# Sums of weights for a seven-product MLP: from VectorE to accumulating DMAs on GpSimd's queue

## The chip, the cores and the metric

The kernel runs on one core of one Trainium2 chip. The metric is the device time of one execution in microseconds (us). Time before: 1537.05 us, the median of three runs (1533.11 to 1542.72).

## The reference, cut to what matters

The whole program is one inference step of a two-layer decoder trunk: a layer with an mLSTM/GLA mixer, a layer with a Mamba-2 mixer, and after each mixer an MLP. 512 prompt tokens and 32 sample tokens (8 sequences of 4) are computed together as 544 columns. The change lies in the MLP, which runs twice:

```python
D_MODEL = 1024; D_FF = 4 * D_MODEL
def _mlp(x, w1, w2):
    return jnp.square(jax.nn.relu(x @ w1)) @ w2
x = _layernorm(DN_ALPHA * x + _mlp(x, P['mlp_w1'][l], P['mlp_w2'][l]), ...)
```

All numbers are float32.

## The kernel before, in words

Activations lie transposed, features on the 128 partitions and tokens along the free axis, in two halves of 272 tokens (TH). A float32 product is made from three float32r products: every operand is split into a high part (a cast to float32r, on ScalarE) and a low part (the rest, a subtraction on VectorE), and TensorE adds high*high, high*low and low*high. For weights the high part is `whi` and the low part `wlo`; a wlo instruction is called lo below.

The 32 blocks of w1 (128 hidden rows each) are done in two ways. Blocks 0 to 5 are done one by one (`dense`, L350). Blocks 6 to 31 are done in 13 **pairs** (m, m+1) by a seven-product scheme (Strassen and Winograd): a pair of weight blocks is a 2x2 matrix a11, a12 (from block m, its two halves over the 1024 features) and a21, a22 (from block m+1), the activations are a 2x2 matrix b11, b21, b12, b22 (feature halves by token halves), and seven products of the size 128 x 512 x 272 replace eight. `quarter` (L498) makes one product: 12 matmuls of 272 columns. `pair` (L556) makes the seven in the order a11, s2, s3, s1, a22, a12, s4 into four PSUM banks: pa (a11, then a12 added), pb (s2), pc (s3, then a22 added), pe (s1, then s4 added). Between them ScalarE copies pa into z (L564), VectorE adds z and the other banks (L567 to L584: z, c22, c21, c12), and `act` (L548) makes Relu and Square on ScalarE and splits the result into hh and hlo, the input of the second matmul.

s1 to s4 are sums of the four weight quarters, made once for each pair in `_pair` (L180): SP's queue loads both blocks (512 KB each) into two buffers wraw; VectorE makes four sums into `wsum` (L191 to L194, each 128 x 512); then four splits follow (L202 the high part on ScalarE, L203 lo on VectorE): a11|a12, s1|s2, s3|s4, a22. `wsum` has one buffer (bufs=1), so the sums of a pair wait until VectorE has read s3|s4 of the pair before. The sums t1 to t4 of activations are made once for each MLP in `take_sums` (L519).

The list `MLP` (L39) sets the order of the work on TensorE: `out` groups of the second matmul (blocks of w2, `dense`, added to the residual by VectorE at L393 or L395) stand between the pairs. Between pairs 8 and 10 and between 10 and 12 there is a short group of 48 matmuls (about 7 us), between the later ones, from 12 to 28, a group of 96 (12 us), and pair 30 follows pair 28 directly. TensorE's order is written out by hand; on the other engines a scheduler at build time orders the instructions. Weights are asked for ahead by `next` (L211): five buffers of whi and wlo, and one lent, so that a pair is split while the pair before it runs. Every engine executes its own queue in order, so a waiting instruction holds all that stand behind it. GpSimd's queue has no instruction in the MLP stages but the sums for LayerNorm (L402, L404: lns) at their ends.

Of the kernel before, what the change touches and what calls it, by code (L numbers as in the profile page):

```python
# [9 lines left out]
F32 = mybir.dt.float32  # L10
F32R = mybir.dt.float32r
U32 = mybir.dt.uint32
AF = mybir.ActivationFunctionType
ALU = mybir.AluOpType
# [3 lines left out]
P = 128  # L18
D = 1024
KT = 8  # L20
# [95 lines left out]
class WeightStream:  # L116
# [63 lines left out]
    def _pair(self, phase, src1, src2):  # L180


        nc = self.nc
        V = nc.vector
        r = []
        for src in (src1, src2):
            r.append(self.raw.tile([P, KT, P], F32, tag="wraw", name="wraw"))
            nc.sync.dma_start(out=r[-1], in_=src)
        sr = self.pairs.tile([P, 4, 4, P], F32, tag="wsum", name="wsum", bufs=1)
        a11, a12, a21, a22 = r[0][:, :4], r[0][:, 4:], r[1][:, :4], r[1][:, 4:]  # L190
        V.tensor_tensor(sr[:, 0], a21, a22, ALU.add)  # L191
        V.tensor_tensor(sr[:, 1], sr[:, 0], a11, ALU.subtract)
        V.tensor_tensor(sr[:, 2], a11, a21, ALU.subtract)
        V.tensor_tensor(sr[:, 3], a12, sr[:, 1], ALU.subtract)  # L194
        out = []
        for x in (r[0], sr[:, 0:2].rearrange("p s k c -> p (s k) c"), sr[:, 2:4].rearrange("p s k c -> p (s k) c"), a22):
            n = x.shape[1]
            kw = {} if n == KT else dict(bufs=1)
            pool = self._pool(phase) if n == KT else self.pairs
            hi = pool.tile([P, n, P], F32R, tag="whi" if n == KT else "w4h", name="whi", **kw)  # L200
            lo = pool.tile([P, n, P], F32R, tag="wlo" if n == KT else "w4l", name="wlo", **kw)
            self.cut[0] = nc.scalar.copy(hi, x).ins  # L202
            self.cut[1] = nc.vector.tensor_tensor(lo, x, hi.bitcast(F32), ALU.subtract).ins  # L203
            out += [(hi[:, k:k + 4], lo[:, k:k + 4]) for k in range(0, n, 4)]
        return dict(zip(("a11", "a12", "s1", "s2", "s3", "s4", "a22"), out))

# [21 lines left out]
def trunk_kernel(ctx, tc, a, stages=("ab", "mlp0", "ssd", "mlp1")):  # L228
    nc = tc.nc
    V, S, G, TE = nc.vector, nc.scalar, nc.gpsimd, nc.tensor  # L230
    cst = ctx.enter_context(tc.tile_pool(name="cst", bufs=1))
# [16 lines left out]
    for st in stages:  # L248
# [10 lines left out]
        else:  # L259
# [3 lines left out]
            for kind, m, *r in MLP:  # L263
                if kind == "pair":
                    ws.plan(st, "pair", a["mlp_w1"][l, m], a["mlp_w1"][l, m + 1])
                else:
                    k, n = m % 8, r[0]
# [8 lines left out]
    ones = cst.tile([P, P], F32, name="ones")  # L276
    V.memset(ones, 1.0)
    epsc = cst.tile([P, 1], F32, name="epsc")
# [3 lines left out]
    def split(hi, lo, src):  # L282
        i = S.copy(hi, src)  # L283
        V.tensor_tensor(lo, src, hi.bitcast(F32), ALU.subtract)  # L284
        return i.ins
# [36 lines left out]
    def launch(gen, lane="norm"):  # L322
        lanes.setdefault(lane, []).append([next(gen), gen])
# [183 lines left out]
    def mlp(l, phase_, outer, xp, out):  # L507

        own = outer.enter_context(ExitStack())
        pool = outer.enter_context(tc.tile_pool(name=phase_, bufs=1, reuse_waits="tile"))
        tp = own.enter_context(tc.tile_pool(name="t" + phase_, bufs=1, reuse_waits="tile"))
        ws.lend(own.enter_context(tc.tile_pool(name="hlt" + phase_, bufs=HLM, reuse_waits="tile")), phase_, HLM)
        ws.pairs = tp
        bt = {}

        def take_sums():  # L519
            b11, b21, b12, b22 = xf[0][:, :4], xf[0][:, 4:], xf[1][:, :4], xf[1][:, 4:]  # L520
            tr = xp.tile([P, KT, TH], F32, tag="lnq", name="tsum", bufs=1)
            ta, tb = tr[:, :4], tr[:, 4:]
            for n in ("t1", "t2", "t3"):
                bt[n] = [tp.tile([P, 4, TH], F32R, name=n + x, bufs=1) for x in "hl"]
            V.tensor_tensor(ta, b12, b11, ALU.subtract)
            V.tensor_tensor(tb, b22, b12, ALU.subtract)
            split(*bt["t1"], ta)
            split(*bt["t3"], tb)
            V.tensor_tensor(ta, b22, ta, ALU.subtract)
            split(*bt["t2"], ta)  # L530
            V.tensor_tensor(tb, b21, ta, ALU.subtract)

            bt["t4"] = [xh[1][:, :4], xl[1][:, :4]]
            split(*bt["t4"], tb)
            bt["b11"], bt["b21"], bt["b22"] = ([x[h][:, k:k + 4] for x in (xh, xl)] for h, k in ((0, 0), (0, 4), (1, 4)))

        hid = {}

        def place(m):
            if m not in hid:  # L540
                hid[m] = (pool.tile([P, T], F32R, tag="hh", name="hh", bufs=8),
                          pool.tile([P, T], F32R, tag="hlo", name="hlo", bufs=8))
            return hid[m]

        def hr():
            return pool.tile([P, TH], F32, tag="hr", name="hr", bufs=6)

        def act(m, hf, x, r=None):  # L548
            c0, c1 = HALVES[hf]
            h = place(m)  # L550
            r = hr() if r is None else r
            S.activation(r, x, AF.Relu)
            S.activation(r, r, AF.Square)
            split(h[0][:, c0:c1], h[1][:, c0:c1], r)

        def pair(m):  # L556
            w = ws.next()
            pa, pb, pc, pe = (x[:, :TH] for x in (psd.tile([P, 512], F32, tag="d", name="psd"), pm("psd"),
                                                  psd.tile([P, 512], F32, tag="d", name="psd"), pm("psd")))
            hp = tc.high_priority  # L560
            z, c22, c21, c12 = (hr() for _ in range(4))
            quarter(w["a11"], bt["b11"], pa, True)
            with hp():
                S.copy(z, pa)  # L564
            quarter(w["s2"], bt["t2"], pb, True)
            with hp():
                V.tensor_tensor(z, z, pb, ALU.add)  # L567
            quarter(w["s3"], bt["t3"], pc, True)
            with hp():
                V.tensor_tensor(c22, z, pc, ALU.add)  # L570
            quarter(w["s1"], bt["t1"], pe, True)
            with hp():
                V.tensor_tensor(c22, c22, pe, ALU.add)
                act(m + 1, 1, c22, c22)
            quarter(w["a22"], bt["t4"], pc, False)
            with hp():
                V.tensor_tensor(c21, z, pc, ALU.add)
                act(m + 1, 0, c21, c21)
            quarter(w["a12"], bt["b21"], pa, False)
            with hp():  # L580
                act(m, 0, pa)
            quarter(w["s4"], bt["b22"], pe, False)
            with hp():
                V.tensor_tensor(c12, z, pe, ALU.add)  # L584
                act(m, 1, c12, c12)

        def hrhs(m):
            def rhs(k, hf):
                c0, c1 = HALVES[hf]
                return hid[m + k][0][:, c0:c1], hid[m + k][1][:, c0:c1]  # L590
            return rhs

        phase(HEADM, xrhs, KT, act, head=HEADM)
        take_sums()
        for kind, m, *r in MLP:
            if kind == "pair":
                if m == 30:
                    ws.lend(None, None, 0)
                pair(m)
                continue  # L600
            n, blocks = r
            if kind == "last":
                own.close()
                ws.lend(outer.enter_context(tc.tile_pool(name="hlx" + phase_, bufs=HLX, reuse_waits="tile")), phase_, HLX)
                end = None if out is None else lambda: last_layernorm(2 * l + 1, xp, out)
                phase(8, hrhs(m), n, residual(False, xp, end), tail=TAIL,
                      after=lambda hf: launch(layernorm(hf, 2 * l + 1, xp, out)) if end is None or hf == 0 else None)
# [12 lines left out]
            if blocks[-1][-1] == 7:  # L620
                for k in range(m, m + n):
                    del hid[k]
# [1155 lines left out]
    n = 0  # L1778
    spill, ahead = a["xT"], None
    left = ctx.enter_context(ExitStack())  # L1780
    while n < len(stages):
        st = stages[n]
        src = spill
        with ExitStack() as stk:
            if st == "ssd":
# [5 lines left out]
                with tc.tile_pool(name="ssd", bufs=1, reuse_waits="tile") as pool:  # L1791
# [4 lines left out]
                    with tc.manual_schedule(engines={mybir.EngineType.PE}):  # L1796
                        out = ssd(pool, ypool, dram, right, ahead, consts)
# [161 lines left out]
```

## Time and profile before

| | |
|---|---|
| median of three runs | 1537.05 us |
| the profiled execution | 1528.88 us, its span 1527.2 us, granted TensorE clock 0.992 |
| TensorE (PE) busy | 1485.8 us, 97% |
| VectorE (DVE) busy | 1091.9 us, 72% |
| ScalarE (ACT) busy | 794.9 us, 52% |
| GpSimd (POOL) busy | 235.8 us, 15% |
| DMA | 172.10 MB, mean 113 GB/s |
| pairs of the first MLP on TensorE | 369 to 636 us |
| pairs of the second MLP on TensorE | 1196 to 1464 us |

How to read the rows that the prediction shows. A row of the timeline has the start in us, the duration in us, the engine, the line, the operation, out<-in with the shape, and in brackets the idle time of the engine just before it and what ended it. Matmuls are pipelined: each row has 0.29 us, but one starts every 0.125 us, so a quarter of 12 takes 1.5 us and a pair of 84 takes 10.5 us. A row of the waits has the waiting engine and line, what it waited for, us in total, times, and the longest. Busy time does not say what a faster engine is worth; that is read from who waits, in the stage.

### The profile page before, as it was taken

The numbers are of one execution on the slowest core, as the hardware profiler recorded it, in microseconds if no ns is written. First come the engines' busy times: TensorE is split into PE (matmuls) and PEld (weight loads), VectorE is DVE, ScalarE is ACT, GpSimd is POOL, SyncE is SP. The second block draws the span as 40 slices with busy tenths as digits, with TensorE's granted clock in tenths as the row PEclk, the third lists the DMA queues.
The fourth block names the chain that finished last, engine by engine and source line by source line (L and its number), as shares of the span: only waits on it lengthen the run. The fifth ranks groups of instructions, "written<-read, shape, count | busy, mean of one in ns | idle before, by whom it ended". The sixth has DMA issues, their size and how long they took to land.

```text
span 1527.2 us, 29115 instructions
## 1 busy us (share of the span) xinstructions
PE 1485.8 (97%) x11611; PEld 1434.4 (94%) x11611; DVE 1091.9 (72%) x2004; ACT 794.9 (52%) x1727; POOL 235.8 (15%) x298
## 2 busy tenths in 40 slices
PE   8999999999999999999999999999999999999997
PEld 7999999899999999999888788989999999999996
DVE  4974476676776677667899988777678677676656
ACT  5644447374444444536786675554347345345343
POOL 0510322010000000022454444420020000000000
PEclk9999999999999999999999999999999999999998
DMA  6321213403333232425457767364222332333221
GB/s 218 96 69 42 101 46 97 174 23 107 99 99 97 84 97 83 142 76 176 118 132 251 228 188 237 97 195 152 72 73 70 94 90 92 97 91 91 69 84 59
DMA packets 81200, 172.10 MB, mean 113 GB/s; under 512 B 9240, under 2 KB 35736, under 8 KB 80808
## 3 DMA queue, kind: packets, MB, share of 16 engines
q1 hardware_dynamic: 52248, 141.20, 29.7%
q10 hardware_dynamic: 26032, 18.29, 4.5%
q0 software_dynamic: 2784, 10.75, 1.8%
q8 instruction: 91, 1.49, 0.4%
q14 instruction: 45, 0.37, 0.1%
HBM read 153.48 MB, written 16.73 MB: 111 GB/s over the span
## 4 chain that ended last, share of the span: by engine, by line
PE 80%; DVE 10%; ACT 4%; DMA 3%; issue 2%; SPq 0%; POOL 0%; ACTq 0%; DVEq 0%
PE psd L361 53%; PE psd L504 17%; DVE wlo L167 2%; ACT whi L166 1%; PE num L749 1%; DVE acc L1442 1%; DMA h0n<-h0n 1%; PE yp L1548 1%; ACT xf L440 1%; PE gs L979 1%; PE it L1595 1%; DVE h0n L1608 1%; PE sp L1526 1%; DMA wraw<-mlp_w 1%; PE ip L1523 1%
## 5 line engine op out<-in xcount | busy, mean ns | idle before, releaser
L361 PE MATMUL psd<-xh,whi 128*128 128x272 f32 x1504 | 447.9, 298 | 9.7 <-ACT xh L283 5.0
L361 PE MATMUL psd<-xh,wlo 128*128 128x272 f32 x1504 | 444.7, 296 | 0.4 <-DVE wlo L167 0.4
L361 PE MATMUL psd<-xl,whi 128*128 128x272 f32 x1504 | 442.2, 294 | 2.5 <-DVE xl L284 2.5
L361 PEld LDWEIGHTS psd<-xh,whi 128*128 128x128 f32 x1504 | 287.1, 191 | 16.8 <-issue 7.7
L361 PE MATMUL psd<-hh,whi 128*128 128x272 f32 x1024 | 296.6, 290 | 4.1 <-DVE xf L395 3.0
L361 PEld LDWEIGHTS psd<-xl,whi 128*128 128x128 f32 x1504 | 287.4, 191 | 9.7 <-DVE xl L284 4.3
L361 PE MATMUL psd<-hh,wlo 128*128 128x272 f32 x1024 | 295.7, 289 | 0.0
L361 PE MATMUL psd<-hlo,whi 128*128 128x272 f32 x1024 | 295.4, 288 | 0.2
L361 PEld LDWEIGHTS psd<-xh,wlo 128*128 128x128 f32 x1504 | 287.0, 191 | 4.4 <-issue 2.6
L167 DVE TENSOR_TENSOR wlo<-wraw,whi 128x1024 fp32r<-128x1024 f32 (+2 forms) x173 | 208.2, 1206 | 65.3 <-ACT whi L166 63.5
L166 ACT CAST whi<-wraw 128x1024 fp32r<-128x1024 f32 (+2 forms) x173 | 174.2, 1011 | 152.3 <-PE psd L361 134.0
L361 PEld LDWEIGHTS psd<-hh,whi 128*128 128x128 f32 x1024 | 192.8, 188 | 6.3 <-DVE xf L395 4.9
L361 PEld LDWEIGHTS psd<-hlo,whi 128*128 128x128 f32 x1024 | 192.8, 188 | 0.7 <-DVE hlo L284 0.6
L361 PEld LDWEIGHTS psd<-hh,wlo 128*128 128x128 f32 x1024 | 192.8, 188 | 0.2
L395 DVE TENSOR_TENSOR xf<-xf,psd 128x272 f32<-128x272 f32 x208 | 88.4, 435 | 77.9 <-PE psd L361 77.4
L504 PE MATMUL psd<-xh,whi 128*128 128x272 f32 x416 | 120.2, 289 | 1.0 <-DVE xf L395 1.0
L504 PE MATMUL psd<-xh,wlo 128*128 128x272 f32 x416 | 119.9, 288 | 0.0
L504 PE MATMUL psd<-xl,whi 128*128 128x272 f32 x416 | 119.6, 288 | 0.0
L202 ACT CAST whi<-wsum 128x1024 fp32r<-128x1024 f32 x52 | 54.3, 1044 | 120.4 <-PE psd L504 72.0
L202 ACT CAST whi<-wraw 128x512 fp32r<-128x512 f32 (+1 forms) x52 | 43.2, 835 | 97.4 <-PE psd L361 83.8
L203 DVE TENSOR_TENSOR wlo<-wsum,whi 128x1024 fp32r<-128x1024 f32 x52 | 63.7, 1225 | 23.1 <-ACT whi L202 23.1
L504 PEld LDWEIGHTS psd<-xh,whi 128*128 128x128 f32 x416 | 78.2, 188 | 1.7 <-DVE xf L395 1.5
(475 smaller groups left out, 2824.5 us busy)
## 6 DMA issues: line engine op xcount, KB each, us to landing
wraw<-mlp_w SPq DMA_DIRECT2D x80, 512.0 KB, 3.7
wraw<-ssd_in SPq DMA_DIRECT2D x40, 512.0 KB, 4.2
wraw<-mlp_w SPq DMA_DIRECT2D x64, 256.0 KB, 3.1
wraw<-ab_in SPq DMA_DIRECT2D x24, 512.0 KB, 3.7
h<-h SPq DMA_DIRECT2D x32, 256.0 KB, 4.3
h0n<-h0n SPq DMA_DIRECT2D x16, 512.0 KB, 4.9
E<-d_cs ACTq DMA_DIRECT2D x16, 512.0 KB, 4.7
s_h<-h0n POOLq DMA_DIRECT2D x16, 512.0 KB, 4.7
```

Source lines behind the costliest of these rows:

```text
L166: nc.scalar.copy(hi[:, r], w[:, r])
L167: nc.vector.tensor_tensor(lo[:, r], w[:, r], hi[:, r].bitcast(F32), ALU.subtract)
L202: self.cut[0] = nc.scalar.copy(hi, x).ins
L203: self.cut[1] = nc.vector.tensor_tensor(lo, x, hi.bitcast(F32), ALU.subtract).ins
L361: last[0] = TE.matmul(ps[:, :TH], wt[:, k, :], rt, start=i == 0, stop=i == n - 1).ins
L395: V.tensor_tensor(x, x, ps, ALU.add)
L440: S.activation(x[:, j], x[:, j], AF.Identity, scale=g[:, j:j + 1], bias=b[:, j:j + 1])
L504: last[0] = TE.matmul(ps, wt[:, k], bt[:, k], start=first and n == 0, stop=n == 11, skip_group_check=not first).ins
L749: TE.matmul(num[i], sT[:, i] if j == i else sT[:, (4, 7, 9)[j] + i - j - 1], vt[key][:, j, h, :w], start=j == 0, stop=j == i)
L979: TE.matmul(p[:, 2 * m * b:2 * m * (b + 1)].rearrange("p (e t) -> p e t", e=2), z[:, 2 * m * b:2 * m * b + P], zq[:, :, m * b:m * (b + 1)] ...
L1442: V.scalar_tensor_tensor(acc[:, :n], ci[:, w:w + n], cw[:, m, w:w + 1], acc[:, :n], ALU.mult, ALU.add)
L1523: TE.matmul(ip[:, j * P:(j + 1) * P], hT[:, j * P:(j + 1) * P], Cf[:, tk], start=True, stop=True)
```

## The change

`_pair` no longer makes the four sums on VectorE. Six DMAs from GpSimd's queue build them in `wsum` from the weights in HBM: two plain copies and four with an addition (`accum_op=ALU.add`), which read the target, add the source and write it back. Because only additions are at hand, the scheme is rewritten with a21 and a22 negated: s1 = a21 + a22, s2 = a21 + a22 + a11, s3 = a21 + a11, s4 = a12 + a11 + a21 + a22. The signs that this turns round are set right in `take_sums` (t1, t2, t4), at z in `pair`, and in `act`, which takes the negative of c21 and c22 by the scale of Relu. SP loads the first block whole (512 KB) as before, but of the second only a22 (256 KB).

```diff
-        V = nc.vector
-        r = []
-        for src in (src1, src2):
-            r.append(self.raw.tile([P, KT, P], F32, tag="wraw", name="wraw"))
-            nc.sync.dma_start(out=r[-1], in_=src)
+        V, G = nc.vector, nc.gpsimd
+        a11, a12, a21, a22 = src1[:, :4], src1[:, 4:], src2[:, :4], src2[:, 4:]
+
+        def twice(x, n=2):
+            return x[:, None].broadcast_to([P, n, 4, P])
         sr = self.pairs.tile([P, 4, 4, P], F32, tag="wsum", name="wsum", bufs=1)
-        a11, a12, a21, a22 = r[0][:, :4], r[0][:, 4:], r[1][:, :4], r[1][:, 4:]
-        V.tensor_tensor(sr[:, 0], a21, a22, ALU.add)
-        V.tensor_tensor(sr[:, 1], sr[:, 0], a11, ALU.subtract)
-        V.tensor_tensor(sr[:, 2], a11, a21, ALU.subtract)
-        V.tensor_tensor(sr[:, 3], a12, sr[:, 1], ALU.subtract)
+        G.dma_start(out=sr[:, 0:3], in_=twice(a21, 3))
+        G.dma_start(out=sr[:, 3], in_=a12)
+        G.dma_start(out=sr[:, 0:2], in_=twice(a22), accum_op=ALU.add)
+        G.dma_start(out=sr[:, 2:4], in_=twice(a11), accum_op=ALU.add)
+        G.dma_start(out=sr[:, 1], in_=a11, accum_op=ALU.add)
+        G.dma_start(out=sr[:, 3], in_=sr[:, 0], accum_op=ALU.add)
+        r = [self.raw.tile([P, KT, P], F32, tag="wraw", name="wraw") for _ in range(2)]
+        nc.sync.dma_start(out=r[0], in_=src1)
+        nc.sync.dma_start(out=r[1][:, 4:], in_=a22)
...
-        for x in (r[0], sr[:, 0:2].rearrange("p s k c -> p (s k) c"), sr[:, 2:4].rearrange("p s k c -> p (s k) c"), a22):
+        for x in (r[0], sr[:, 0:2].rearrange("p s k c -> p (s k) c"), sr[:, 2:4].rearrange("p s k c -> p (s k) c"), r[1][:, 4:]):
...
-            V.tensor_tensor(ta, b12, b11, ALU.subtract)
+            V.tensor_tensor(ta, b11, b12, ALU.subtract)
...
-            V.tensor_tensor(ta, b22, ta, ALU.subtract)
+            V.tensor_tensor(ta, b22, ta, ALU.add)
...
-            V.tensor_tensor(tb, b21, ta, ALU.subtract)
+            V.tensor_tensor(tb, ta, b21, ALU.subtract)
...
-        def act(m, hf, x, r=None):
+        def act(m, hf, x, r=None, sign=1.0):
...
-            S.activation(r, x, AF.Relu)
+            S.activation(r, x, AF.Relu, scale=sign)
...
-                V.tensor_tensor(z, z, pb, ALU.add)
+                V.tensor_tensor(z, z, pb, ALU.subtract)
...
-                act(m + 1, 1, c22, c22)
+                act(m + 1, 1, c22, c22, -1.0)
...
-                act(m + 1, 0, c21, c21)
+                act(m + 1, 0, c21, c21, -1.0)
```

Lines of the changed kernel are four higher from `take_sums` on, and L202 and L203 become L206 and L207. The scheduler orders the engines anew. GpSimd's queue has 156 rows more, six for each of the 26 pairs. For the second pair of the first MLP they stand like this, with what each waits for (DMASW are the completions of GpSimd's own DMAs, DVE the last reading of wsum by VectorE):

```order
L190 DMA wsum<-mlp_w 128x3x512 [waits DMASW5_49,DMASW4_49,DVE_49]
L191 DMA wsum<-mlp_w 128x512
L192 DMA wsum<-mlp_w 128x2x512 [waits DMASW6_49]
L193 DMA wsum<-mlp_w 128x2x512 [waits DMASW7_49]
L194 DMA wsum<-mlp_w 128x512 [waits DMASW0_49]
L195 DMA wsum<-wsum 128x512 [waits DMASW1_49]
```

The third waits for the first, the fourth for the second, the fifth for the third and the sixth for the fourth: what was four instructions on VectorE is a chain of three landings. For the first pair of an MLP the six stand ahead of the additions for the LayerNorm before it (L402, now L406).

On ScalarE the splits keep their places in most pairs. Around pair 10 of the first MLP, where pair 12's s1|s2 and s3|s4 are cast (COPY is pair 10's z), there stood before:

```order
L202 CAST whi<-wsum 128x1024
L564 COPY hr<-psd 128x272
L202 CAST whi<-wsum 128x1024
L552 ACTIVATE hr<-hr 128x272
L202 CAST whi<-wraw 128x512
```

and now:

```order
L568 COPY hr<-psd 128x272
L206 CAST whi<-wsum 128x1024
L556 ACTIVATE hr<-hr 128x272
L557 ACTIVATE hr<-hr 128x272
L206 CAST whi<-wsum 128x1024
L206 CAST whi<-wraw 128x512
L287 CAST hh<-hr 128x272
L556 ACTIVATE hr<-hr 128x272
L166 CAST whi<-wraw 128x1024
L556 ACTIVATE hr<-psd 128x272
```

Pair 12's first cast has moved behind pair 10's copy of z, and both stand ahead of the Relu from PSUM (the last row) that frees bank pa. One pair earlier nothing moved: pair 10's first cast still stands directly ahead of pair 8's copy of z.

On VectorE the sums are gone. At the end of the first MLP, where pair 28 runs and pair 30 is split, there stood before (L567 is z of pair 28, L570 and L573 c22, L577 c21):

```order
L203 TENSOR_TENSOR wlo<-wsum,whi 128x1024
L567 TENSOR_TENSOR hr<-hr,psd 128x272
L570 TENSOR_TENSOR hr<-hr,psd 128x272
L573 TENSOR_TENSOR hr<-hr,psd 128x272
L577 TENSOR_TENSOR hr<-hr,psd 128x272
```

and now:

```order
L207 TENSOR_TENSOR wlo<-wsum,whi 128x1024
L571 TENSOR_TENSOR hr<-hr,psd 128x272
L207 TENSOR_TENSOR wlo<-wsum,whi 128x1024
L574 TENSOR_TENSOR hr<-hr,psd 128x272
L577 TENSOR_TENSOR hr<-hr,psd 128x272
```

The second lo of pair 30 (s3|s4) has moved in between z and c22 of pair 28. The end of the second MLP reads the same.

More of the change, by code (lines that the diff above doesn't have):

```diff
@@ L202, in _pair @@
             self.cut[0] = nc.scalar.copy(hi, x).ins
-            self.cut[1] = nc.vector.tensor_tensor(lo, x, hi.bitcast(F32), ALU.subtract).ins
+            self.cut[1] = V.tensor_tensor(lo, x, hi.bitcast(F32), ALU.subtract).ins
             out += [(hi[:, k:k + 4], lo[:, k:k + 4]) for k in range(0, n, 4)]
```

## The prediction

> **What bounds the kernel now.** I read the page's engine line first, then the table by stage over both MLPs, then PE's waits in those stages. The engine line (busy us, share, instructions):
>
> ```profile
> span 1527.2 us, 29115 instructions
> PE 1485.8 (97%) x11611; PEld 1434.4 (94%) x11611; DVE 1091.9 (72%) x2004; ACT 794.9 (52%) x1727; POOL 235.8 (15%) x298
> ```
>
> PE has 41 us left. The stages with pairs, first MLP then second (stretch, its length, busy PE, PEld, DVE, ACT, POOL, clock, DMA share, GB/s):
>
> ```profile
> 397.00:434.00 37.00, 35.02 (x272) 34.06 (x270) 26.80 (x50) 18.73 (x37) 0.00 (x0) 1.00 0.31 97
> 434.00:603.00 169.00, 168.94 (x1344) 168.89 (x1345) 116.27 (x203) 75.65 (x143) 0.00 (x0) 1.00 0.30 92
> 1225.00:1261.00 36.00, 34.41 (x268) 33.43 (x266) 26.50 (x49) 18.37 (x37) 0.00 (x0) 1.00 0.32 97
> 1261.00:1430.00 169.00, 168.26 (x1339) 168.01 (x1340) 116.31 (x202) 75.39 (x142) 0.00 (x0) 1.00 0.30 92
> ```
>
> In the long stretches PE is busy 168.94 and 168.26 of 169 us at clock 1.00, so the DVE work that the change removes there is already covered. What PE waits for from 369 to 636 us (two rows) and from 1196 to 1464 us (two rows):
>
> ```profile
> PE psd L361 <- DVE xf L395: 1.3, 1, 1.3
> PE psd L504 <- DVE xf L395: 0.6, 1, 0.6
> PE psd L361 <- DVE xf L395: 1.8, 2, 1.3
> PE psd L504 <- DVE xf L395: 0.4, 1, 0.4
> ```
>
> Together 4.1 us. That is all a faster DVE can win in these stages.
>
> **What goes.** Four sums per pair, 26 pairs:
>
> ```profile
> L191 DVE TENSOR_TENSOR wsum<-wraw x26: 683/692/696, 348.4 to 1432.0; 128x512 f32<-128x512 f32 x26
> L194 DVE TENSOR_TENSOR wsum<-wraw,wsum x26: 684/687/693, 352.3 to 1437.0; 128x512 f32<-128x512 f32 x26
> ```
>
> 104 x 0.69 = 72 us leave DVE, and 4.1 us of it was on PE's path: -4.1 us at best, which I take whole, since the late xf adds of 413 to 434 us stand behind these sums. Signs in take_sums, pair and act change no count and no shape: nothing.
>
> **What comes: a chain of DMAs.** Per pair, GpSimd issues D1 (768 KB), D2 (256 KB), then accumulates D3 and D4 (512 KB each), D5 and D6 (256 KB each). D3 waits for D1 to land, D5 for D3, D6 for D4 and D3. The cast of s1|s2 needs D1, D3, D5: three landings in a row. I call c the time from D1's start to D5's landing; D6 lands about 1 us later (an estimate: one more transfer of 256 KB on the same queue). No accumulating DMA is in the trace. The nearest rows (KB each, median us from issue to landing; then the issue on POOL in ns and the spread for 512 KB):
>
> ```profile
> wraw<-mlp_w SPq DMA_DIRECT2D x80, 512.0 KB, 3.7
> wraw<-mlp_w SPq DMA_DIRECT2D x64, 256.0 KB, 3.1
> wraw<-mlp_w SPq DMA_DIRECT2D x16, 128.0 KB, 2.3
> s_h<-h0n POOLq DMA_DIRECT2D x16, 512.0 KB, 4.7
> spill<-xf POOLq DMA_DIRECT2D x2, 1088.0 KB, 5.1
> L1609 POOL DMA_DIRECT2D s_h<-h0n x16: 531/594/599, 803.4 to 1017.1; - x16
> DMA to landing us min/median/max: 2.9/4.7/7.7
> ```
>
> From below, each transfer at its cheapest: 2.9 + 2.9 + 2.3 = 8.1 us. From above, each at POOL's slowest: 3 x 7.7 = 23.1 us. I take POOL's medians, and count an accumulate as twice its bytes because it reads its target too: D1 4.9 (between 4.7 and 5.1), D3 as 1024 KB 5.1, D5 as 512 KB 4.7, and 0.5 for the hand-overs (an estimate): **c = 15.2 us**. Bytes: 26 x (2560 + 768 - 1024) KB = 61 MB more, on engines that are at a 0.30 share in these stages; SP's weight loads may land later, but ACT waits 5 us for PE before it casts them (479.41 in the next fence).
>
> The Trainium skill (Collectives: The Full Stack, section "The bandwidth ceiling") says that adding in flight costs no cycles but needs two source reads on one ring, which halves the rate. Priced as plain copies instead, D3 and D5 would be 4.7 and about 3.1, and c 13.2; no run here shows which.
>
> **Where the chain must fit.** wsum has one buffer, so D1 of the next pair starts when DVE has read s3|s4 of the pair before. In steady state (start, us, engine; PE rows are two pairs' first matmuls):
>
> ```profile
> 456.73 0.29 PE L504 MATMUL psd<-xh,whi 128*128 128x272 f32 x1
> 467.03 1.23 DVE L203 TENSOR_TENSOR wlo<-wsum,whi 128x1024 fp32r<-128x1024 f32 x1 [0.61 <-ACT whi L202]
> 479.34 0.29 PE L504 MATMUL psd<-xh,whi 128*128 128x272 f32 x1
> 479.41 1.05 ACT L202 CAST whi<-wraw 128x1024 fp32r<-128x1024 f32 x1 [5.00 <-PE psd L361]
> 485.43 1.05 ACT L202 CAST whi<-wsum 128x1024 fp32r<-128x1024 f32 x1 [3.99 <-PE psd L504]
> ```
>
> Free at 467.03 + 1.23 = 468.3, cast at 485.4, where it waits for PE anyway: **17.2 us**, in a period of 22.6. With c = 15.2 it fits, and costs nothing. Beyond 17.2 each microsecond lengthens every period, in 7 chains per MLP, 14 in all, since the Relu that frees the pair's first bank (ACT) and c12 (DVE) stand behind that cast and its lo.
>
> At the start the pairs stand closer, with short groups between them:
>
> ```profile
> 385.41 1.23 DVE L203 TENSOR_TENSOR wlo<-wsum,whi 128x1024 fp32r<-128x1024 f32 x1 [0.51 <-ACT whi L202]
> 397.87 1.05 ACT L202 CAST whi<-wsum 128x1024 fp32r<-128x1024 f32 x1 [3.47 <-PE psd L361]
> 399.51 0.39 ACT L564 COPY hr<-psd 128x272 f32<-128x272 f32 x1 [0.59 <-PE psd L504]
> 402.51 0.44 DVE L570 TENSOR_TENSOR hr<-hr,psd 128x272 f32<-128x272 f32 x1 [1.00 <-PE psd L504]
> 403.81 0.29 PE L504 MATMUL psd<-xh,whi 128*128 128x272 f32 x1
> 408.90 1.22 DVE L203 TENSOR_TENSOR wlo<-wsum,whi 128x1024 fp32r<-128x1024 f32 x1
> 416.25 0.39 PE L504 MATMUL psd<-xh,whi 128*128 128x272 f32 x1
> 434.06 0.39 PE L504 MATMUL psd<-xh,whi 128*128 128x272 f32 x1 [0.61 <-DVE xf L395]
> 463.76 0.42 ACT L552 ACTIVATE hr<-hr 128x272 f32<-128x272 f32 x1
> 464.32 0.62 ACT L202 CAST whi<-wraw 128x512 fp32r<-128x512 f32 x1
> 466.90 0.39 ACT L552 ACTIVATE hr<-psd 128x272 f32<-128x272 f32 x1
> ```
>
> Pair 10: wsum is free at 386.6, and its cast still stands ahead of pair 8's copy of z on ACT. Behind it come cast 1.05, lo 1.23, and z and c22 at 0.44 each, 3.2 us with gaps, until PE may begin the a22 quarter, which it wants at 403.8. So c up to 14.0 is free, and PE stalls **c - 14.0 = 1.2 us**.
>
> Pair 12: free at 410.1. Its cast now stands behind the copy of z (see the order above), but nine ACT rows, 5.9 us by these durations (casts 1.05, 1.05, 1.05 and 0.62; four Relu, Square and hh casts at 0.42), run from it through the Relu (0.39) that frees pair 10's first bank. PE wants that bank in the second short tile, 11.3 us after 416.25, at 427.6. So c up to 11.5 is free, and PE stalls **c - 11.5 = 3.7 us**. Pair 14 starts its chain 4.2 us after that cast and may be late by 7.6 us after 434.06 (shifted by the stalls): c - 15.9, nothing here.
>
> At the end pair 30 follows pair 28 directly:
>
> ```profile
> 602.86 1.23 DVE L203 TENSOR_TENSOR wlo<-wsum,whi 128x1024 fp32r<-128x1024 f32 x1 [0.61 <-ACT whi L202]
> 615.13 0.29 PE L504 MATMUL psd<-xh,whi 128*128 128x272 f32 x1
> 621.14 0.29 PE L504 MATMUL psd<-xh,whi 128*128 128x272 f32 x1
> ```
>
> Free at 604.1; on DVE both lo's of pair 30 now stand ahead of pair 28's c22, so the a22 quarter of 621.1 needs D6 (c + 1), cast, lo and c22 (2.8 us): c up to 13.2 is free, PE stalls **c - 13.2 = 2.0 us**.
>
> GpSimd's queue: pair 6's six DMAs stand ahead of the additions for the first LayerNorm's sums, but POOL idles there longer than a chain:
>
> ```profile
> 294.76 1.68 POOL L402 TENSOR_TENSOR lns<-xf 128x272 f32<-128x272 f32 x1 [30.17 <-DVE xf L393]
> ```
>
> The 30 us cover it; without them POOL would be late by up to c, and PE with it. All other chains meet an empty queue (POOL 0.00 busy in the four stretches).
>
> **The sum.** Per MLP 1.2 + 3.7 + 2.0 = 6.9, twice 13.8, less 4.1: +9.7 us. The profiled execution took 1528.88 us (span 1527.2), so 1538.6; the median of the runs shown is 1537.05, 8.2 above it, so **1546.8 us**.
>
> **Rivals.** (1) *The chain outlasts the period.* For it: three landings in a row, accumulates unseen so far, and single POOL transfers of 7.7 us. Against it: at medians 2 us are left. From c = 17.2 every chain pays. At c = 20 an MLP pays 6.0 + 8.5 + 4.1 + 6.8 + 7 x 2.8 = 45.0, two pay 90, less 4.1: 1623 us. At 23.1 it is 79 per MLP, 1691 us. (2) *Only the tight places pay more*, c from 16.1 to 17.2: 10 to 14 per MLP, 1553 to 1561 us. (3) *A short chain*, c under 11.5: no stall at all, and the 4.1 us come back, 1533 us. For it: POOL's cheapest 512 KB took 2.9 us, and the MLP stages have quieter DMA than those where the 4.7 was taken. The Trainium skill (DMA: Bandwidth & Descriptors, "Anatomy of one DMA") states about 2.0 us plus bytes at 436 GB/s for a DMA from GpSimd; by that c would be about 11, on the side of this rival, while the 4.7 us median here lies above that rule's 3.2. (4) *Faster by over 1%*: DVE relief would have to win 15 us where PE's waits show 4.1; only a cause outside these rows could do it.
>
> **How the numbers follow.** The forecast (c from 11.5 to 16.1) has 0.37, its own range 1533 to 1552; rival 1 has 0.32, rival 2 0.10, rival 3 0.17, rival 4 0.04. About 1% (15 us) is what a measurement of this kernel can tell from no change. Within it lie the forecast and rival 3: 0.54; slower are rivals 1 and 2: 0.42; faster 0.04. For 8 in 10 the range goes from 1530, a little under rival 3, to 1640, which is c = 20.8 (54 per MLP): it leaves out the long end of rival 1.
>
> **What would show it.** DVE's busy time falls by about 72 us and PE's does not. The landing times of wsum's DMAs give c directly: D1 near 4.9, D3 near 5.1, D5 near 4.7. ACT's casts of wsum wait for PE in the long stretches (right) or for a DMA (rival 1). PE's idle time grows at pairs 8 to 12 and at pair 28, by 2 to 7 us per MLP, with the copy of z or a Relu as its cause. The forecast is wrong if PE waits in every pair, if POOL's issue takes several times 0.59 us, or if PE's idle time shrinks by more than 4 us.

## The result, and the profile after

The changed kernel takes 1619.72 us (median of four runs, 1616.18 to 1623.25), the kernel before 1535.08 us (four runs). The ratio is 1.0544, 95% interval 1.0492 to 1.0596: 5.4% slower. The range of the prediction, 1530 to 1640 us, holds it; the forecast that was called likeliest, 1546.8 us with no stall in the steady pairs, did not come. What came is its rival 1, "the chain outlasts the period", which stood at 1623 us for c = 20.

The profiled execution took 1616.24 us, 87.4 more than the one before. The head of the page, the engine line, GpSimd's own DMA queue and the chain that ended last:

```profile
span 1614.5 us, 29346 instructions
PE 1513.1 (94%) x11611; PEld 1451.7 (90%) x11611; DVE 1028.2 (64%) x1900; ACT 793.0 (49%) x1727; POOL 378.5 (23%) x454
...
q0 software_dynamic: 31904, 78.92, 22.1%
...
PE 50%; DMA 28%; DVE 8%; ACT 8%; issue 5%; POOL 1%; SPq 0%; ACTq 0%; DVEq 0%; POOLq 0%
```

Read two things off the engine line. DVE lost 63.7 us of busy time and the kernel is slower all the same. (The forecast's 72 us is the sum of the durations. Rows that follow each other on DVE overlap, two sums of 0.69 us start at 432.36 and 432.97, and busy time counts the overlap once.) And PE, with the same 11611 matmuls, is busy 27.3 us *longer* (1485.8 before), while its idle time (span less busy) grew from 41.4 to 101.4 us, by 60.0. The two add up to the whole loss of 87.3 us: two thirds are waits, one third is a slower TensorE.

The stages of the first MLP (stretch, length, PE, PEld, DVE, ACT, POOL, clock, DMA share, GB/s): pairs 6 to 12, pairs 12 to 28, pairs 28 and 30.

```profile
373.50:442.00 68.50, 60.71 (x452) 59.62 (x450) 28.92 (x51) 21.20 (x40) 15.42 (x16) 0.95 0.72 172
442.00:652.00 210.00, 194.94 (x1478) 190.51 (x1479) 113.42 (x201) 87.84 (x168) 48.68 (x52) 0.98 0.74 181
652.00:680.50 28.50, 23.40 (x175) 23.18 (x174) 13.16 (x21) 13.25 (x25) 1.74 (x2) 0.94 0.48 107
```

Before, PE was busy 168.94 of 169 us in the long stretch. Now 15 us of 210 are idle there, and the clock is below 1.00 in all three rows.

Who waits: the largest rows of PE, then those of ACT (the longest in the last column).

```profile
PE psd L508 <- DVE hr L574: 22.1, 4, 6.5
PE psd L365 <- DVE hr L581: 18.4, 11, 2.8
PE psd L365 <- DVE xf L397: 12.9, 3, 8.4
```

```profile
ACT whi L206 <- DMA wsum<-mlp_w: 146.5, 17, 13.7
...
ACT whi L206 <- DMA wsum<-wsum: 40.1, 6, 9.9
```

L574 and L581 are c22 and c21, DVE's additions that free PSUM banks. PE names DVE, but DVE only stands behind a lo, the lo behind a cast on ACT, and the cast now waits for a DMA 23 times. Before, the casts of this line waited for PE (the largest row):

```profile
ACT whi L202 <- PE psd L361: 132.3, 30, 8.5
```

One steady chain on GpSimd's queue (start, duration of the issue, line, and the wait ahead of it), then the two casts of wsum on ACT, and on PE the matmul that waited at that time (with the longer wait at 417.65 that is used further below):

```profile
494.16 0.79 POOL L190 DMA_DIRECT2D wsum<-mlp_w  x1 [7.19 <-DVE wlo L207]
494.94 0.59 POOL L191 DMA_DIRECT2D wsum<-mlp_w  x1
499.52 1.24 POOL L192 DMA_DIRECT2D wsum<-mlp_w  x1 [4.00 <-DMA wsum<-mlp_w]
500.27 1.74 POOL L193 DMA_DIRECT2D wsum<-mlp_w  x1
507.75 0.89 POOL L194 DMA_DIRECT2D wsum<-mlp_w  x1 [5.74 <-DMA wsum<-mlp_w]
510.43 0.85 POOL L195 DMA_DIRECT2D wsum<-wsum  x1 [1.79 <-DMA wsum<-mlp_w]
519.72 0.79 POOL L190 DMA_DIRECT2D wsum<-mlp_w  x1 [8.43 <-DVE wlo L207]
```

```profile
514.10 1.05 ACT L206 CAST whi<-wsum 128x1024 fp32r<-128x1024 f32 x1 [9.08 <-DMA wsum<-wsum]
...
517.12 1.04 ACT L206 CAST whi<-wsum 128x1024 fp32r<-128x1024 f32 x1
```

```profile
417.65 0.39 PE L508 MATMUL psd<-xh,whi 128*128 128x272 f32 x1 [4.69 <-DVE hr L574]
...
516.80 0.39 PE L365 MATMUL psd<-hh,whi 128*128 128x272 f32 x1 [1.68 <-DVE hr L581]
```

Read it as a **ring**. D1 starts at 494.16, D3 at 499.52 when D1 has landed, D5 at 507.75 when D3 has, D6 at 510.43 when D4 has. The first cast, at 514.10, waits for D6 (the only DMA wsum<-wsum, which completes s4): in this chain and in the next the scheduler has put the cast of s3|s4 ahead of that of s1|s2, which follows at 517.12; in the other steady chains of this MLP s1|s2 comes first and waits for D5. Then comes the lo of the second cast, and at 519.72 the buffer is free and the next D1 starts. That is 19.9 us to the first cast and 5.6 us more: 25.6 us round the ring, where TensorE needs 22.6 for a period. Over the seven steady chains of the first MLP whose first cast waited for a DMA (pair 14 and pairs 18 to 28) the time from D1's start to that cast is 17.7 to 20.8 us, 19.4 in the mean. To D5's landing, which is the prediction's c, it is 17.6 to 19.9 us, 18.9 in the mean.

### The profile page after: what moved, and what is told of

It reads as the page before. It is cut to its first block, busy times and chain, and to the rows that moved or that the text cites. A ratio compares the mean times of both kernels' runs of the same rounds, so it can differ in the third digit from the quotient of the medians.

```text
span 1614.5 us, 29346 instructions
## 1 busy us (share of the span) xinstructions
PE 1513.1 (94%) x11611; PEld 1451.7 (90%) x11611; DVE 1028.2 (64%) x1900; ACT 793.0 (49%) x1727; POOL 378.5 (23%) x454
## 2 busy tenths in 40 slices
DMA packets 110321, 233.46 MB, mean 145 GB/s; under 512 B 11736, under 2 KB 38232, under 8 KB 109928
## 3 DMA queue, kind: packets, MB, share of 16 engines
q0 software_dynamic: 31904, 78.92, 22.1%
## 4 chain that ended last, share of the span: by engine, by line
PE 50%; DMA 28%; DVE 8%; ACT 8%; issue 5%; POOL 1%; SPq 0%; ACTq 0%; DVEq 0%; POOLq 0%
PE psd L365 38%; DMA wsum<-mlp_w 24%; PE psd L508 3%; ACT whi L206 2%; DVE wlo L207 2%; DMA wsum<-wsum 2%; PE num L753 1%; DMA E<-d_cs 1%; PE yp L1552 1%; ACT whi L166 1%; ACT xf L444 1%; ACT hr L556 1%; PE gs L983 1%; PE it L1599 1%; PE sp L1530 1%
## 5 line engine op out<-in xcount | busy, mean ns | idle before, releaser
L365 PE MATMUL psd<-xh,whi 128*128 128x272 f32 x1504 | 446.7, 297 | 15.4 <-DVE xf L397 8.4
L365 PE MATMUL psd<-hh,whi 128*128 128x272 f32 x1024 | 306.5, 299 | 34.5 <-DVE hr L581 18.4
L365 PEld LDWEIGHTS psd<-xh,whi 128*128 128x128 f32 x1504 | 285.9, 190 | 22.9 <-issue 13.2
L365 PE MATMUL psd<-hlo,whi 128*128 128x272 f32 x1024 | 300.0, 293 | 0.2
L365 PE MATMUL psd<-hh,wlo 128*128 128x272 f32 x1024 | 300.1, 293 | 0.0
L167 DVE TENSOR_TENSOR wlo<-wraw,whi 128x1024 fp32r<-128x1024 f32 (+2 forms) x173 | 209.2, 1212 | 65.6 <-ACT whi L166 63.7
L365 PEld LDWEIGHTS psd<-hh,whi 128*128 128x128 f32 x1024 | 197.3, 193 | 45.3 <-DVE hr L581 20.9
L365 PEld LDWEIGHTS psd<-hlo,whi 128*128 128x128 f32 x1024 | 197.5, 193 | 0.7 <-DVE hlo L288 0.6
L365 PEld LDWEIGHTS psd<-hh,wlo 128*128 128x128 f32 x1024 | 197.3, 193 | 0.2
L206 ACT CAST whi<-wsum 128x1024 fp32r<-128x1024 f32 x52 | 54.2, 1043 | 223.7 <-DMA wsum<-mlp_w 146.5
L207 DVE TENSOR_TENSOR wlo<-wsum,whi 128x1024 fp32r<-128x1024 f32 x52 | 63.7, 1225 | 141.1 <-ACT whi L206 141.0
L508 PE MATMUL psd<-xh,whi 128*128 128x272 f32 x416 | 123.1, 296 | 22.1 <-DVE hr L574 22.1
L190 POOL DMA_DIRECT2D wsum<-mlp_w x26 | 20.7, 797 | 325.9 <-DVE wlo L207 280.0
```

Source lines behind the costliest of these rows:

```text
L167: nc.vector.tensor_tensor(lo[:, r], w[:, r], hi[:, r].bitcast(F32), ALU.subtract)
L190: G.dma_start(out=sr[:, 0:3], in_=twice(a21, 3))
L207: self.cut[1] = V.tensor_tensor(lo, x, hi.bitcast(F32), ALU.subtract).ins
L365: last[0] = TE.matmul(ps[:, :TH], wt[:, k, :], rt, start=i == 0, stop=i == n - 1).ins
L508: last[0] = TE.matmul(ps, wt[:, k], bt[:, k], start=first and n == 0, stop=n == 11, skip_group_check=not first).ins
```

## The experiments

Ratios are taken against runs of the kernel before on the same chip (median 1531.65 us for experiments 1 to 4, 1531.71 us for 5, 6 and 8).

### 1. Two buffers for the sums

```diff
-        sr = self.pairs.tile([P, 4, 4, P], F32, tag="wsum", name="wsum", bufs=1)
+        self.odd = not self.odd
+        if self.odd:
+            sr = self.pairs.tile([P, 4, 4, P], F32, tag="wsum", name="wsum", bufs=1)
+        else:
+            sr = self.xp.tile([P, KT, TH], F32, tag="lnq", name="wsum", bufs=1).rearrange("p k c -> p (k c)")
+            sr = sr[:, :16 * P].rearrange("p (s k c) -> p s k c", s=4, k=4)
```

> The changed kernel with a second buffer for the sums: every other pair builds them in the tile that holds the activation sums and the LayerNorm squares, which lies idle between the pairs. The chain of a pair can start a whole period earlier; DMAs, bytes and the work of every engine stay the same. Theory A (the one buffer makes a ring: six DMAs of about 19 us, then two casts and two lo's of about 5 us, which is longer than the 22.6 us that TensorE needs for a period): pairs 14 to 28 start 22.6 us apart again, ScalarE's casts of the sums wait for TensorE and not for a DMA, and what stays is the 4.3 us by which the first pair came later and a few us at pair 10: 1535 to 1555 us. Theory B (the DMA traffic itself, or its adding, slows the other engines or their loads): the periods stay at 24 to 25 us, 1595 to 1620 us.

Measured: 1534.53 us (10 runs), ratio to before 1.001 (0.9988 to 1.0032). The whole loss is gone, with the same 233.46 MB. Pairs 12 to 28 start 22.6 us apart. The steady stretch of this kernel (columns as above), and ACT's waits in the pairs of the first MLP:

```profile
449.00:608.00 159.00, 159.00 (x1268) 159.00 (x1267) 94.30 (x164) 71.36 (x136) 40.93 (x44) 1.00 0.83 203
```

```profile
ACT whi L206 <- PE psd L365: 55.6, 13, 5.0
ACT whi L206 <- PE psd L508: 35.9, 9, 4.0
```

PE is busy all of 159 us at clock 1.00 while the DMA engines are at a share of 0.83 and 203 GB/s, more than in the changed kernel (0.74, 181). So it is not the traffic: theory A holds. Nor has the chain become shorter: from D1's start to D5's landing it takes 18.8 us here and 18.6 in the changed kernel (medians of 26 chains). It was the one buffer that turned the DMAs' latency into a period. From the copy of z of the first pair to that of the last an MLP now takes 254.4 and 254.1 us (before 256.8 and 257.0): 5.2 us less in all, for which the prediction had 4.1. Against experiment 6, which has the same signs and its sums on DVE (256.5 and 256.3), it is 4.2 us.

### 2. Copies in place of additions

```diff
-        G.dma_start(out=sr[:, 0:2], in_=twice(a22), accum_op=ALU.add)
+        G.dma_start(out=sr[:, 0:2], in_=twice(a22))
...
```

and likewise the other three.

> The changed kernel with the four accumulating DMAs as plain copies of the same shapes, in the same order and with the same waits; s1 to s4 are then not sums, and the output is another. Theory A1 (adding makes a DMA slow, since it reads its target as well): the third and fourth DMA land after about 5 us and not 8.0, the fifth and sixth after 3.5 us, the chain takes about 15 us, pairs 14 to 28 start 22.6 us apart, and the time is 1540 to 1560 us. Theory A2 (the length of the chain comes from the queue, the issue on GpSimd and the number of landings, whatever the operation): the third lands after 7 to 8 us as before and the time stays at 1605 to 1620 us.

Measured: 1550.49 us (4 runs), ratio 1.0108 (1.0066 to 1.0149). D3's landing, in the changed kernel and then with copies (issue on POOL in ns, least, median and most; then the landing):

```profile
L192 POOL DMA_DIRECT2D wsum<-mlp_w x26: 1222/1237/1240, 270.5 to 1519.3; - x26
...
DMA to landing us min/median/max: 5.5/7.2/13.0
```

```profile
L192 POOL DMA_DIRECT2D wsum<-mlp_w x26: 712/712/714, 275.2 to 1457.6; - x26
...
DMA to landing us min/median/max: 3.7/4.8/8.7
```

The medians of D1, D3, D4, D5, D6 were 5.2, 7.2, 9.7, 5.2, 3.6 us; with copies they are 5.1, 4.8, 6.0, 4.1, 3.3. From D1's start to D5's landing, hand-overs included, the median is 15.5 us, under the 17.2 of the window (18.6 in the changed kernel), and twelve of the sixteen periods from pair 12 to pair 28 are 22.5 to 22.7 us again: theory A1. The queue's own row shows the price of adding:

```profile
q0 software_dynamic: 21920, 78.92, 14.8%
```

For the same 78.92 MB the packets took 14.8% of 16 engines over 1547.8 us, 3665 us, against 22.1% over 1614.5, 5709 us. The 2044 us between them belong to the 40.9 MB that are added (26 x 1.5 MB): 50 us for a MB on top of the 46 that a MB costs when it is copied. **An added byte holds the DMA engines 2.1 times as long as a copied one.** The Trainium skill (Collectives: The Full Stack, section "The bandwidth ceiling") says that an addition in flight needs two source reads and so halves the rate; the trace agrees, 2.1 times here. It also takes longer to issue: 1.24 us for D3 and 1.74 for D4 on POOL against 0.71 and 0.73 for the copies.

### 3. The traffic alone

```diff
+        t = self.xp.tile([P, KT, TH], F32, tag="lnq", name="sink", bufs=1).rearrange("p k c -> p (k c)")
...
+        with self.tc.issue_after(self.was) if self.was is not None else nullcontext():
+            V.memset(t[:, 2, 0, 0:1], 0.0)
+        G.dma_start(out=t[:, 0:3], in_=twice(b21, 3))
...
```

in the kernel before, with the other five DMAs into the same tile.

> The kernel before, sums on VectorE, and beside it the six DMAs of each pair into a tile that nobody reads; a write of one element by VectorE, which stands behind the lo of the pair before, lets the chain of each pair start where it starts in the changed kernel. It has all the traffic of the changed kernel (and 6.5 MB more of loads on SP's queue), and nothing waits for the sums. Theory A (only waiting for the chain costs): the pairs keep their 22.6 us, the first pair of each MLP comes up to 4.3 us later because the first chain shares the DMA engines with the reload of the residual, 1535 to 1548 us. Theory B (the traffic costs): periods of 24 us and more, 1580 to 1620 us.

Measured: 1583.14 us (4 runs), ratio 1.033 (1.0305 to 1.0355). This looks like theory B, but DVE's waits show that the experiment was not clean:

```profile
DVE sink L182 <- DMA sink<-sink: 48.9, 11, 9.5
```

The small write by DVE, meant only to pace the chain, itself waited for the sixth DMA of the chain before, 11 times, up to 9.5 us, with the sums standing behind it. The stalls lie in the close pairs at the start of an MLP; of the later periods most are 22.6 to 23.1 us. The run tells nothing about traffic alone; experiment 1 does, with the same bytes for the chains.

### 4. One buffer cut in two

```diff
-        sr = self.pairs.tile([P, 4, 4, P], F32, tag="wsum", name="wsum", bufs=1)
+        s12, s34 = (self.pairs.tile([P, 2, 4, P], F32, tag=t, name="wsum", bufs=1) for t in ("s12", "s34"))
...
+        for dst, src, kw in ((s12, twice(a21), {}), (s34[:, 0], a21, {}), (s34[:, 1], a12, {}),
...
```

> The changed kernel with the one buffer of the sums cut in two, one for s1 and s2 and one for s3 and s4, each given free by its own lo; the first copy is cut in two for it, seven DMAs and no more memory. The next chain starts when the lo of s1 and s2 is done, about 3 us earlier. Theory A (the ring of chain, cast and lo sets the period): the ring for s1 and s2 is 19 us of DMAs, a cast of 1.05 and a lo of 1.23 with hand-overs, 21.5 to 22 us, just under the 22.6 us of TensorE; pairs 14 to 28 start 22.6 to 23.2 us apart, some 10 to 15 us per MLP come back while the losses at pairs 8 to 12 and at pair 30 mostly stay: 1575 to 1605 us. Theory B (traffic): no change, 1610 to 1625 us.

Measured: 1569.54 us (4 runs), ratio 1.0245 (1.0198 to 1.0292), a little better than theory A said. In the first MLP the six periods from pair 14 to pair 26 are 22.6 to 24.4 us (theory A had 22.6 to 23.2), the next, to pair 28, is 27.6, and the way from the first copy of z to the last is 272.1 us, against 296.8 in the changed kernel and 256.8 before. Giving the halves of the buffer free separately gives back more than half of the loss, with no more memory and no less traffic.

### 5. The first pair's sums on DVE, two buffers for the rest

```diff
+        if not self.first:
+            G.dma_start(out=sr[:, 0:3], in_=twice(a21, 3))
...
+        if self.first:
+            V.tensor_tensor(sr[:, 0], b21, b22, ALU.add)
...
```

> The changed kernel with the two buffers of the experiment before, and the four sums of the first pair of each MLP made by VectorE (with plus signs) from weights that SP loads; the other twelve pairs keep their DMAs. In the changed kernel the first pair's chain ran beside the reload of the residual (14.4 us to landing against 8.1), TensorE waited 8.4 us for it against 2.8, and the first pair came 4.3 us later. Theory A (that chain shares the DMA engines with the reload): the reload lands after about 8 us again, the wait falls to about 3 us, and the time is 1523 to 1529 us, 3 to 6 us under the two buffers alone and as much under the kernel before. Theory B (the reload is late for another reason): 1530 to 1535 us, no change to the two buffers alone.

Measured: 1527.42 us (12 runs), ratio to before 0.997 (0.9953 to 0.9987): the one version here that beats the kernel before, by 0.3%, little but outside its interval. It is 7.1 us under the two buffers alone, and theory A holds. PE's wait for the residual's first additions, 250 to 375 us of the changed kernel and 250 to 385 of this one (its L410 is L397 there):

```profile
PE psd L365 <- DVE xf L397: 8.4, 1, 8.4
```

```profile
PE psd L378 <- DVE xf L410: 2.1, 1, 2.1
```

The reload of the residual (xf<-xT, 544 KB) lands after 6.4 us at the median, against 14.4 in the changed kernel.

### 6. The signs alone

```diff
-        V.tensor_tensor(sr[:, 1], sr[:, 0], a11, ALU.subtract)
+        V.tensor_tensor(sr[:, 1], sr[:, 0], a11, ALU.add)
...
```

> The kernel before, its sums still on VectorE and one buffer, but in the form with plus signs only: the same number of instructions of the same shapes. Theory A (the signs cost nothing): within 0.3 % of before, 1527 to 1537 us. A rival (the scale of Relu, the turned order of operands or the new order on VectorE cost something): 1540 us and more.

Measured: 1532.68 us (10 runs), ratio 1.0011 (0.9994 to 1.0028). The signs cost nothing that can be measured.

### 7. The fifth DMA ahead of the fourth

```diff
-        G.dma_start(out=sr[:, 2:4], in_=twice(a11), accum_op=ALU.add)
         G.dma_start(out=sr[:, 1], in_=a11, accum_op=ALU.add)
+        G.dma_start(out=sr[:, 2:4], in_=twice(a11), accum_op=ALU.add)
```

> The changed kernel with the fifth DMA ahead of the fourth in GpSimd's queue, so that the third (512 KB, adding) runs without the fourth beside it. If the third takes 8.2 us because the fourth shares the engines with it: it lands after 5 to 6.5 us. If an adding DMA of 512 KB takes 8 us by itself: 7.5 us or more. The fourth is issued only after the third has landed, so the sixth comes later, at about 24 us after the start, and s3|s4 sets the ring: 24 and 3.5 to 5 us, periods of 27 to 29 us and 1650 to 1720 us by either.

Measured (one run): 1617.82 us, and in the trace the queue stands as in the changed kernel: the scheduler put the fourth back ahead of the fifth. So this was the changed kernel once more and tested nothing. The same with the order fixed by a chain of issue_after:

> The changed kernel with the fifth DMA ahead of the fourth in GpSimd's queue, this time with the order of the six fixed, so that the third (512 KB, adding, 7.2 us to landing at the median in the changed kernel) runs without the fourth beside it. If the third is slow because the fourth shares the engines with it: it lands after 5 to 6 us. If an adding DMA of 512 KB takes 7 us by itself: 6.5 us or more. The fourth, issued about 7 us later than before and alone with the fifth, lands after 6 to 8 us and not 9.7. s3|s4 is then ready some 24 us after the start of the chain and sets the ring with its cast and lo (2.5 us): periods of 26 to 28 us and 1650 to 1710 us in all, slower than the changed kernel by either.

Measured (one run): 1702.13 us. D3, then D5 with D4 behind it, then D6:

```profile
487.63 1.24 POOL L195 DMA_DIRECT2D wsum<-mlp_w  x1 [4.38 <-DMA wsum<-mlp_w]
493.81 2.14 POOL L195 DMA_DIRECT2D wsum<-mlp_w  x2 [4.95 <-DMA wsum<-mlp_w]
502.83 0.89 POOL L195 DMA_DIRECT2D wsum<-wsum  x1 [6.88 <-DMA wsum<-mlp_w]
```

In the chain shown D5 starts 493.81 - 487.63 = 6.2 us after D3, when D3 has landed, but this chain is one of the quick ones. Over the 26 chains the median from D3's start to D5's is 7.1 us, and D3's landing 6.8; in the changed kernel, with D4 beside it, they are 7.45 and 7.2. So D4 costs D3 some 0.4 us, and of the two expectations the second holds: D3 is slow without D4. That does not make 7 us the price of the operation: in experiment 1 D3 has D4 beside it and lands after 5.7 us in the median (more on this below). D4 without D3 takes about 8.1 us (493.81 + 0.9 to 502.83) and not 9.7. The time is as expected, since the order puts four landings into a row for s4; the periods, most of them near 30 us, are longer than the 26 to 28 expected.

### 8. The last two additions on DVE, one buffer

```diff
-        G.dma_start(out=sr[:, 1], in_=a11, accum_op=ALU.add)
-        G.dma_start(out=sr[:, 3], in_=sr[:, 0], accum_op=ALU.add)
...
+        V.tensor_tensor(sr[:, 1], sr[:, 1], r[0][:, :4], ALU.add)
+        V.tensor_tensor(sr[:, 3], sr[:, 3], sr[:, 0], ALU.add)
```

> The changed kernel with one buffer, the fifth and sixth addition (a11 to s2, and s1 to s4) made by VectorE, 52 sums of 0.69 us (36 us more work than the changed kernel, 36 us less than before). Two landings in a row and not three: ring 5.4 + 8.2 + 0.7 + 5 = 19 to 20 us, under the 22.6 us of a period. Theory A (the length of the ring decides): pairs 14 to 28 start 22.6 us apart, the places at the start and the end of an MLP cost 0 to 5 us each, 1538 to 1565 us. Rival (VectorE, which now waits in its order for a landing ahead of the residual's additions, holds TensorE up): periods over 23.5 us, 1580 us and more.

Measured: 1609.61 us (4 runs), ratio 1.0525 (1.0499 to 1.0552). Theory A missed by 45 us and the rival came. PE's first wait, and DVE around it:

```profile
PE psd L508 <- DVE hr L574: 48.7, 22, 4.9
```

```profile
502.61 0.69 DVE L198 TENSOR_TENSOR wsum<-wsum 128x512 f32<-128x512 f32 x1 [3.83 <-DMA wsum<-mlp_w]
503.22 0.43 DVE L399 TENSOR_TENSOR xf<-xf,psd 128x272 f32<-128x272 f32 x1
503.57 1.22 DVE L207 TENSOR_TENSOR wlo<-wraw,whi 128x1024 fp32r<-128x1024 f32 x1
504.70 0.43 DVE L571 TENSOR_TENSOR hr<-hr,psd 128x272 f32<-128x272 f32 x1
505.24 0.44 DVE L574 TENSOR_TENSOR hr<-hr,psd 128x272 f32<-128x272 f32 x1
```

L198 (s1 into s4) waits for D4 at the head of DVE's queue, and the running pair's z and c22, on which PE waits in 22 of 26 pairs, stand behind it. A ring that would fit is of no use when its wait stands in the wrong place of an engine's order.

## Why the prediction was right or wrong

**DVE's relief: right.** It is small because PE hardly waited for DVE: 4.2 to 5.2 us (experiment 1) for 4.1 forecast. **The signs: right** (experiment 6).

**The length of the chain: the step that failed.** The prediction put D1 at 4.9, D3 at 5.1, D5 at 4.7 and hand-overs at 0.5: c = 15.2, inside the window of 17.2. In the seven steady chains the mean from D1's start to D3's is 5.55, from D3's to D5's 7.73, and D5 lands 5.6 later: c = 18.9, outside it. Most of the miss is D3. Twice the bytes was the right rule for the engines' time (2.1, experiment 2), but it was turned into a landing time by a row of 1088 KB that is a plain copy (spill, 5.1 us). The adding makes D3 longer: 7.2 us in the median, 4.8 as a copy (experiment 2). What goes with the rest is not so much D4 (experiment 7) as SP's weight loads on the same DMA engines; the prediction asked whether the chain delays those loads, not whether they delay the chain. Queue q1, SP's (packets, MB, share of the engines), in the first 5.5 us of D3 in the chain shown, where D5 follows after 8.2 us, and then in pair 12's chain (from 431.36), where it follows after 6.0:

```profile
q1 hardware_dynamic: 334, 0.60, 34.9%
```

```profile
q1 hardware_dynamic: 152, 0.26, 12.5%
```

In the median over 26 chains the other queues move 0.62 MB in these 5.5 us in the changed kernel, and 0.25 MB in experiment 1, where D3 lands after 5.7 us. No run takes SP's loads away, so their part is read off and not isolated.

That the length of the ring is the cause, and not the operation as such or the traffic, is shown from three sides: copies (c 15.5) give 1550 us, and the two MLPs are 6.8 us longer than before (first to last copy of z), where the forecast for c = 15.2 had 9.7; a buffer given free earlier gives 1570; a second buffer gives 1535 with c as long as before (18.8).

**The window of 17.2 us and the tight places: right in kind, not shown in size.** PE lost time in the steady pairs and at each of the tight places. With the 19.4 us to the first cast put for c into the prediction's own terms, against the starts of the pairs on PE in the first MLP (before, after):

| from pair to pair | before | after | longer by | term at c = 19.4 |
|---|---|---|---|---|
| 6 to 8 | 28.62 | 33.29 | 4.7 | none |
| 8 to 10 | 18.45 | 23.68 | 5.2 | c - 14.0 = 5.4 |
| 10 to 12 | 17.81 | 23.87 | 6.1 | c - 11.5 = 7.9 |
| 12 to 14 | 22.67 | 24.91 | 2.2 | c - 15.9 = 3.5 |
| 14 to 28, seven | 158.4 | 173.3 | 14.9 | 7 x (c - 17.2) = 15.4 |
| 28 to the end of 30 | 21.07 | 27.94 | 6.9 | c - 13.2 = 6.2 |
| sum | 267.0 | 307.0 | 40.0 | 38.4 |

The sum fits to 1.6 us, but that is luck in part. With c = 18.9 the terms come to 32.7, and with the c of each pair's own chain (17.9 at pair 10, 16.1 at pair 12, 15.7 at pair 30) to 24. The terms let each chain start where it started before, while in a ring a late cast makes the next chain start late too; they leave out the first row, in which PE waits 2.9 us for L397; and they know nothing of the clock (below), which the table measures along with the waits. What the steady pairs do show is the ring: from D1 of pair 16 (471.12) to D1 of pair 30 (643.79) seven rings take 24.7 us each, and PE's seven periods 24.8.

**Pair 6's chain: wrong.** The prediction checked GpSimd's queue, which was free as it said, but not the DMA engines: they reload the residual at that time. PE waited 8.4 us there instead of 2.8, the first pair came 4.3 us later (its copy of z at 375.20 instead of 370.89), and experiment 5, which takes the chain away, takes the wait away (2.1). The wait is the sure part. The time of the first copy of z scatters by more: over the kernels of this study it is 370.9 to 374.2 without that chain ahead of it or with the chain later, and 373.5 to 380.0 with it.

**What was not in the forecast at all: the clock after a wait.** PE in the changed kernel (columns as above) around a wait of 4.7 us, around the 1.68 us at 516.80, and behind a wait of 2.5 us that ended at 543.25:

```profile
413.00:416.00 3.00, 0.00 (x0) 0.00 (x0) 0.51 (x1) 1.33 (x2) 0.85 (x1) 1.00 0.73 128
416.00:419.00 3.00, 1.34 (x8) 1.35 (x9) 1.94 (x4) 0.79 (x2) 0.00 (x0) 0.87 0.04 6
419.00:422.00 3.00, 3.00 (x16) 3.00 (x16) 1.44 (x3) 1.99 (x5) 0.00 (x0) 0.56 0.02 5
422.00:425.00 3.00, 3.00 (x26) 3.00 (x25) 2.26 (x4) 2.93 (x6) 0.00 (x0) 1.00 0.54 164
...
514.00:517.00 3.00, 1.32 (x10) 1.10 (x10) 1.82 (x3) 2.85 (x6) 0.00 (x0) 1.00 0.00 0
517.00:520.00 3.00, 3.00 (x24) 2.85 (x23) 2.51 (x5) 3.00 (x7) 0.28 (x1) 1.00 0.51 165
...
544.60:547.90 3.30, 3.30 (x17) 3.30 (x16) 3.27 (x5) 3.27 (x9) 1.37 (x2) 0.50 0.69 178
```

After the long wait the granted clock is 0.56 for three us and only 16 matmuls start in them, not 24 to 26; after the short one it stays 1.00; after the one of 2.5 us it is 0.50 for 3.3 us. The Trainium skill (TensorE: Matmul & The Clock Gate, "Part 1: The HAM clock gate") states that the clock falls to a half after an idle window of about 3.4 us and needs about as long of work to come back; the trace agrees on the half and on the way back, but here 2.5 us of waiting were enough. So a long wait is paid about one and a half times: over the whole kernel 60.0 us of idle time brought 27.3 us of longer busy time.

**The accounts.** First pair 4.3, first MLP 40.0, between the MLPs 4.4, second MLP 38.7 (copies of z): 87.4 us. The 4.4 us between the MLPs are not explained by the change: over the kernels of this study that stretch took 569.2 to 576.8 us (570.65 before, 575.05 changed, 570.3 with two buffers, 576.8 in experiment 5), so it scatters by as much.

**The chances.** 0.42 for slower and 0.32 for rival 1 said that the matter was open; the weight on the forecast rested on medians of other stages, with a margin of 2.0 us in 17.2. Two of its signs of being wrong came: the casts waited for a DMA, and GpSimd's issue took 1.24 and 1.74 us, two to three times 0.59. The figure of about 11 under rival 3 stands for 10.1 with plain bytes and 11.9 with the doubled ones, so only the first lay under that rival's bound of 11.5.

## What to carry to other kernels

Work moved from a busy engine to a chain of DMAs trades throughput for latency: add up the landings of the chain, each with what runs beside it, and the work that gives its buffer free, and compare that ring with the period; if it is within some us, give it a second buffer (a tile that lies idle at that time will do) before anything else. Check a moved transfer against the other transfers of its time too, not against its queue alone. And price a wait of TensorE of several us at about one and a half times its length (an estimate: against the kernel before, each us of added idle time brought 0.4 to 0.9 us of added busy time in the slower kernels of this study).

## What the runs showed of the hardware

- An adding DMA from GpSimd's queue holds the DMA engines 2.1 times as long as a copy of the same bytes; 512 KB land after 7.2 us as the first of two and 9.7 as the second (as copies 4.8 and 6.0), 6.8 without the second; with two buffers, where fewer other loads run beside it, the first lands after 5.7. All are medians of 26.
- Its issue takes GpSimd 1.24 to 1.74 us for 512 KB (copies 0.71 to 0.73) and 0.89 for 256 KB (0.57).
- DMA traffic at a share of 0.83 and 203 GB/s did not slow TensorE: 159.00 of 159.00 us busy at clock 1.00.
- More idle time of TensorE goes with a lower clock, with a scatter of some us of busy time. Span less busy time, busy time, mean granted clock for the same 11611 matmuls: before 41.4, 1485.8, 0.992; first pair on DVE (experiment 5) 39.7, 1491.7, 0.987; copies 52.5, 1495.3, 0.985; cut buffer 68.5, 1507.3, 0.979; changed 101.4, 1513.1, 0.974; fifth first 163.1, 1537.3, 0.956.
